# Modulation products in four column quarters at once, and indivisible blocks of matmuls, in a two-block transformer kernel

## The chip, the cores and the metric

The kernel runs on one core of one Trainium2 chip. The metric is device time in microseconds (us) of one execution. The core's engines work side by side from instruction lists of their own: TensorE (PE, matmuls; its weight loads are shown as PEld), VectorE (DVE), ScalarE (ACT), GpSimd (POOL) and SyncE (SP, which here issues all transfers). They wait for each other through semaphores.

## The reference

The program chains two blocks of two layers each on 512 tokens of width 1024. What matters here are three parts of it:

```python
# first block, second layer: stick-breaking attention, 16 heads of 64
logits = einsum('bhtd,bhsd->bhts', q, k) * SCALE
log_keep = where(mask, log_sigmoid(-logits), 0)
later = cumsum(log_keep, reverse=True) - log_keep
a = where(mask, exp(log_sigmoid(logits) + later), 0)
out = einsum('bhts,bhsd->bhtd', a, v)

# second block, both layers: modulation from two condition vectors c and c_ctx
m = silu(cvec) @ ada_w[i] + ada_b[i]            # (1024) x (1024, 3072)
shift, scale, gate = split(m, 3)

# second block, first layer: latent attention, 16 heads, 512 tokens + 256 context tokens
p = softmax(einsum('bqhgd,bkhd->bhgqk', q, k) * scale)
o = einsum('bhgqk,bkhv->bqhgv', p, v)
```

All values are float32.

## The kernel before

The whole program is unrolled: `layer0`, `layer1`, `mla` and `diff` are traced one after the other into five instruction lists. A scheduler of the framework then orders each engine's list by its own estimate of when operands are ready and sets all semaphores; so the order on an engine is not that of the Python text. Tiles come from pools; a tag with `bufs=n` has n buffers, and whoever takes a buffer waits for the last reader of its earlier content.

PSUM has one bank `mm` (`p_mm`) and one bank `pv` (`p_pv`) in the stages spoken of here, two `tr` banks for transposes (`p_tr`), and two double banks `lg` for logits (`p_lg`). Weights arrive in three buffers of 512 KB with the tag `wraw`; ACT rounds one into a high part `wh`, POOL subtracts to get the low part `wl` (lines 126 and 127), and most products run as three matmuls (lines 147 to 149).

Two stages carry the change. In the **stick stage** (`layer1`, `stick_steps`) `pipeline` walks through 24 steps, three for each pair of heads c: logits on PE (lines 684 to 686), sigmoids on ACT, a running product on DVE (line 695), a product on POOL (line 698), and two steps later transposes on PE (`aT_p`, line 172) and, at each pair's third step, the products of probabilities and values: eight float32 matmuls (line 726), which alternate between the lower and the upper 64 columns of the PE array (e = 0 and 1) and accumulate in `pv`. In the **latent stage** (`mla`, `mla_steps`) there are 80 steps, five for each head: logits (lines 147 to 149), softmax over ACT, DVE and POOL (lines 1073 to 1075 and 1036), transposes (`PT_p`), and after every second head the products with the values for both heads: 12 matmuls 64x512, then 4 matmuls 64x256 into `pv` again (line 1057), with the same two column halves in turn. Between the steps `pipeline` puts pieces of other work, gates and projections that use `mm` among them.

The modulation vectors are such pieces. There are six parts q (three for each layer of the second block), three in each stage. A part takes eight blocks k of 128 weight rows. `ada_piece` loads one block (`araw`, 512 KB, a `wraw` buffer) and multiplies it with the 32 columns of `cs[:, k, :]`, two of which hold the condition vectors, in two float32 matmuls of 512 columns (line 768). Even blocks use column quarters 0 and 1 of the PE array, odd ones 2 and 3; all eight blocks accumulate in one `pv` bank. DVE copies the bank to SBUF once (line 772), and small matmuls with `asel` add the quarters (line 775). In the trace each float32 matmul that is no transpose has two records of one form.

Of the kernel before, what the change touches and what calls it, by code (L numbers as in the profile page):

```python
# [10 lines left out]
F32 = mybir.dt.float32  # L11
F32R = mybir.dt.float32r
BF16 = mybir.dt.bfloat16
AF = mybir.ActivationFunctionType
ALU = mybir.AluOpType
# [4 lines left out]
P = 128  # L20
# [3 lines left out]
NT = S // P  # L24
# [5 lines left out]
FREE = 10 ** 6  # L30
# [11 lines left out]
class Block:  # L42
    def __init__(self, ctx, tc, a, out):
        self.ctx, self.tc, self.nc, self.a, self.out = ctx, tc, tc.nc, a, out
        self.nc.scalar.preload_act_table_set("natural_log_exp_and_others")
        self.st = ""
        self.last_pair = None
        self.pools = {}
        self.open_pools = {}
        self.cp = self.open("consts")  # L50
        self.wp = self.open("weights")
        self.sm = self.open("small")
        self.ps = self.open("psum", space=PSUM)
        self.dr = ctx.enter_context(tc.tile_pool(name="scratch", bufs=1, space=DRAM))
        self.xs = self.dr.tile([S, D], F32, name="xs")
        self.xs2 = self.dr.tile([S, D], F32, name="xs2")
        self.xf = self.dr.tile([NK, P, S], F32, name="xf")
        self.gates = self.dr.tile([2, 2, 2, 512], F32, name="gates")
        self.wq = []
        self.w_dma = self.w_split = self.w_next = 0  # L60
# [465 lines left out]
    def layer1(self):  # L526
        nc, a = self.nc, self.a
# [9 lines left out]
        ks, qs, vtok = [], [], [lp.tile([P, D], F32, name=f"vtok{t}") for t in range(NT)]  # L537
# [16 lines left out]
        og, pieces, steps = {}, [], []  # L554
# [12 lines left out]
        for c in range(NK):  # L567
            pieces.append((c + 1, lambda c=c: z_piece(c), 3 * c + 3))
        for q in range(3):
            n = 6 * q + 3  # L570
            pieces += self.ada_pieces(q, [n + k // 2 for k in range(8)])
        for c in range(NK):
            steps += self.stick_steps(c, ks, qs, vtok, og, ap)
        self.pipeline(steps, 2, pieces)
# [69 lines left out]
    def stick_steps(self, c, ks, qs, vtok, ogs, pool):  # L644


        nc = self.nc
# [54 lines left out]
        def second(n, segs):  # L702
            aT, bt = h["aT"], h["bt", n]
            b0, pr = 0, None
            for e, i, o in segs:
                if b0 + i + 1 > 4:
                    b0, pr = 0, None
                if pr is None:
                    pr = self.p_tr("aT_p")
                for j in range(i + 1):  # L710
                    self.transpose(pr[:, (b0 + j) * P:(b0 + j + 1) * P], bt[:, o + j * P:o + (j + 1) * P])
                src = pr[:, b0 * P:(b0 + i + 1) * P].rearrange("p (j t) -> p j t", t=P)
                if i == 3:
                    nc.scalar.copy(aT[e][:, 3 * i:4 * i + 1, :], src)
                else:
                    nc.vector.tensor_copy(out=aT[e][:, 3 * i:4 * i + 1, :], in_=src)
                b0 += i + 1
            if n < 2:
                return
            self.need(c + 1)  # L720
            pv = self.p_pv("pv1")
            for j in range(NT):
                for e in range(2):
                    hd = 2 * c + e
                    av = aT[e][:, 4 * j:10 + j:3, :]
                    nc.tensor.matmul(pv[64 * e:64 * e + 64, j * P:], lhsT=vtok[j][:, hd * 64:(hd + 1) * 64], rhs=av, start=(j == 0), stop=(j == NT - 1))
            og = ogs[c // 2][:, (c % 2) * 512:(c % 2 + 1) * 512]
            nc.vector.tensor_tensor(out=og, in0=pv, in1=og, op=ALU.mult)

# [2 lines left out]
        self.last_pair = h  # L732
        tiles = [[(0, 3, 0), (0, 2, 512), (0, 0, 896)], [(1, 3, 0), (1, 2, 512), (1, 0, 896)], [(0, 1, 0), (1, 1, 512)]]
        return [(lambda n=n, t=t: first(n, t), lambda n=n, t=t: second(n, t)) for n, t in enumerate(tiles)]


# [16 lines left out]

    def ada_pieces(self, q, steps):

        return [(FREE, lambda k=k: self.ada_piece(q, k), n) for k, n in enumerate(steps)]

    def ada_piece(self, q, k):
        nc = self.nc
        layer, part = divmod(q, 3)  # L760
        if k == 0:
            self.ada_ps = self.p_pv("ada_p")
        ps = self.ada_ps
        raw = self.wp.tile([P, 1024], F32, tag="wraw", name="araw", bufs=3)
        nc.sync.dma_start(out=raw, in_=self.a["ada_w_2"][layer, k * P:(k + 1) * P, part * 1024:(part + 1) * 1024])
        for b in range(2):
            j = 2 * (k % 2) + b
            nc.tensor.matmul(ps[32 * j:32 * j + 32, :], lhsT=self.cs[:, k, :], rhs=raw[:, b * 512:(b + 1) * 512], start=(k < 2), stop=(k >= 6), tile_position=(0, 32 * j))  # L768
        if k < 7:
            return  # L770
        row = self.wp.tile([P, 1024], F32R, tag="wh", name="ada_row", bufs=4).bitcast(F32)
        nc.vector.tensor_copy(out=row[:, :512], in_=ps)
        pr = self.p_tr("ada_t")
        for t in range(4):
            nc.tensor.matmul(pr[:, 4 * t:4 * t + 4], lhsT=row[:, t * P:(t + 1) * P], rhs=self.asel, start=True, stop=True)
        b0 = self.col["ada_b"] + 8 * q
        for v in range(2):
            nc.vector.tensor_tensor(
                out=self.ada[:, v, 8 * q:8 * q + 8].rearrange("p (b t) -> p b t", t=4),
                in0=pr[:, :16].rearrange("p (t b v) -> p v b t", b=2, v=2)[:, v],  # L780
                in1=self.vec[:, b0:b0 + 8].rearrange("p (b t) -> p b t", t=4), op=ALU.add)
        if part == 1:
            nc.vector.tensor_scalar(out=self.ada1[:, :, 8 * layer:8 * layer + 8], in0=self.ada[:, :, 8 * q:8 * q + 8], scalar1=1.0, scalar2=None, op0=ALU.add)
        if part == 2:
            pr = self.p_tr("ada_g")
            nc.tensor.matmul(pr[:4, :], lhsT=self.asel, rhs=row[:, :512], start=True, stop=True)
            nc.vector.tensor_copy(out=row[:4, 512:], in_=pr[:4, :])
            for b in range(2):
                nc.sync.dma_start(out=self.gates[layer, :, b], in_=row[2 * b:2 * b + 2, 512:])
# [48 lines left out]
    def mla(self):  # L838
        nc, a = self.nc, self.a
# [12 lines left out]
        raws = [p0.tile([P, 768], F32, tag="lraw", name="lraw", bufs=3) for _ in range(3)]  # L852
# [44 lines left out]
        V = lambda g, ns: [(8 * g + 1, lambda i=i: self.mla_v(g, i, grp, kvlat, self.pools["mla1"]), n) for i, n in enumerate(ns)]  # L897
# [20 lines left out]
        pieces, steps = [], []  # L918
        pieces = V(0, [0, 1, 2])
        for g in range(4):  # L920
            n = 20 * g
# [1 line left out]
            if g < 3:  # L923
                pieces += V(g + 1, [n + 6, n + 7, n + 9]) + K(2 * g + 2, n + 10, n + 11) + Q(g + 1, [n + 12, n + 13, n + 14, n + 14, n + 15, n + 16])
        for q in range(3, 6):
            pieces += self.ada_pieces(q, [20 * q - 38 + k for k in range(8)])
        self.chain = []
        for h in range(16):
            steps += self.mla_steps(h, grp, kTs, og, ogc, pool)
# [68 lines left out]
    def mla_steps(self, h, grp, kTs, og, ogc, pool):  # L998
        nc = self.nc
        g, hh, e = h // 4, h % 4, h % 2  # L1000
        H = {}
# [39 lines left out]
        def second(qb):  # L1041
            for pe, dst, i in H[qb]:
                self.probs_T(pe, dst, i)
            if qb < 4:
                return
            if e == 0:
                return
            c = h // 2
            H0 = H["prev"]
            self.need(8 * g + 1)  # L1050
            V = grp["V", g]
            for nk, n, k0, px, o in ((6, 512, 0, "pt", og[c]), (2, 256, 4, "ptc", ogc[c])):
                pv = self.p_pv("pv2")[:, :n]
                for k in range(nk):
                    for ee, HH in ((0, H0), (1, H)):
                        vs = slice((hh - 1 + ee) * 64, (hh + ee) * 64)
                        nc.tensor.matmul(pv[64 * ee:64 * ee + 64, :], lhsT=V[:, k0 + k, vs], rhs=HH[px][:, k, :], start=(k == 0), stop=(k == nk - 1))  # L1057
                nc.vector.tensor_tensor(out=o, in0=pv, in1=o, op=ALU.mult)

        if self.chain:  # L1060
            self.chain[-1]["next"] = prep
            H["prev"] = self.chain[-1]
        self.chain.append(H)
        return [(lambda q=q: first(q), lambda q=q: second(q)) for q in range(5)]

    def soft(self, L, pool, W, bufs):
# [432 lines left out]
```

## Time and profile before

| | |
|---|---|
| runs of the kernel before | 1595.2, 1595.64 (median), 1601.13 us |
| the profiled execution's own time | 1594.69 us |
| its span, first to last instruction | 1592.9 us |
| PE, DVE, ACT, POOL busy | 95%, 58%, 46%, 38% of the span |
| stick stage with the pieces (383 to 547 us) | 164 us, PE busy 148.44 us |
| latent stage with the pieces (787 to 1057 us) | 270 us, PE busy 265.76 us |
| mean granted TensorE clock | 0.983 of full speed |

Times in the rows are counted from the span's start. A matmul's record begins where its data start to stream and ends at a modelled end, so records of neighbours overlap: what a matmul costs is read from one start to the next, and a run of like matmuls from its total busy time. An engine that is not busy may just have nothing to do; only a wait on the engine that ends the stage costs time.

### The profile page before, as it was taken

How to read it: one execution, taken by the hardware profiler on the slowest of the kernel's cores; microseconds unless marked ns; L12 is line 12 of the kernel's file. 1: busy time of each engine (PE TensorE's matmuls, PEld its weight loads, DVE VectorE, ACT ScalarE, POOL GpSimd, SP SyncE). 2: the span in 40 equal slices, each digit the busy share in tenths (PEclk: the TensorE clock that was granted, in tenths of full speed). 3: DMA queues.
4: the chain of work that ended last, by engine and by line, in shares of the span. 5: the costliest groups of instructions: out<-in, count | busy, mean ns of one | idle time of the engine just before them, and what ended most of it. 6: DMA issues, size and time to landing. Idle time of an engine off the chain costs nothing.

```text
span 1592.9 us, 24439 instructions
## 1 busy us (share of the span) xinstructions
PE 1505.3 (95%) x9590; PEld 1253.3 (79%) x9590; DVE 927.9 (58%) x1769; ACT 733.8 (46%) x1347; POOL 603.4 (38%) x431
## 2 busy tenths in 40 slices
PE   6999999999899899999999999999798999999997
PEld 4777889997555678888876657579697999999987
DVE  6676465523766656442465566546866555556576
ACT  5323344436566433332565455543235554555642
POOL 2534555553444453212333222435442324343310
PEclk9999999999999999999999999999898999999999
DMA  5322432223244334311103030425421112111122
GB/s 157 105 79 89 123 118 83 98 84 115 81 132 133 106 120 124 87 44 50 50 1 120 5 120 2 145 80 186 132 69 55 41 41 67 40 56 52 54 74 100
DMA packets 149747, 136.01 MB, mean 85 GB/s; under 512 B 12612, under 2 KB 135224, under 8 KB 149632
## 3 DMA queue, kind: packets, MB, share of 16 engines
q1 hardware_dynamic: 149632, 134.45, 27.3%
q8 instruction: 76, 1.25, 0.3%
q14 instruction: 39, 0.32, 0.1%
HBM read 126.02 MB, written 8.40 MB: 84 GB/s over the span
## 4 chain that ended last, share of the span: by engine, by line
PE 41%; DVE 6%; ACT 5%; issue 3%; DMA 2%; POOL 1%; SPq 0%; DVEq 0%; POOLq 0%; ACTq 0%
PE PT_p L172 5%; PE pv L1057 4%; PE qkv_p L147 2%; PE qkv_p L149 2%; PE qkv_p L148 2%; PE pv L1420 2%; PE gt_p L147 2%; PE gt_p L148 2%; PE gt_p L149 2%; PE lg L147 2%; PE lg L148 2%; PE lg L149 2%; PE ada_p L768 1%; ACT pe L1074 1%; DMA wraw<-in_out_w_dram 1%
## 5 line engine op out<-in xcount | busy, mean ns | idle before, releaser
L127 POOL TENSOR_TENSOR wl<-wraw,wh 128x1024 fp32r<-128x1024 f32 (+2 forms) x159 | 376.4, 2376 | 379.5 <-ACT wh L126 366.3
L126 ACT CAST wh<-wraw 128x1024 fp32r<-128x1024 f32 (+2 forms) x164 | 166.4, 1020 | 281.2 <-issue 57.9
L1074 ACT ACTIVATE pe<-lg,st 128x768 f32<-128x768 f32 x160 | 130.5, 816 | 76.7 <-DVE st L1073 60.6
L1073 DVE TENSOR_REDUCE st<-lg 128x1 f32<-128x768 f32 x160 | 133.9, 845 | 38.4 <-PE lg L1401 20.1
L1036 POOL TENSOR_SCALAR pe<-pe,st 128x768 f32<-128x768 f32 (+1 forms) x96 | 73.6, 767 | 159.2 <-DVE st L1075 154.0
L147 PE MATMUL qkv_p<-wh,h 128*128 128x256 f32 x384 | 109.9, 286 | 0.8 <-ACT V L1346 0.7
L172 PEld LDWEIGHTS PT_p<-ident,pe 128*128 128x128 f32 x640 | 72.3, 142 | 47.8 <-issue 16.5
L149 PE MATMUL qkv_p<-wh,h 128*128 128x256 f32 x384 | 108.6, 283 | 0.2 <-DVE h L217 0.2
L148 PE MATMUL qkv_p<-wl,h 128*128 128x256 f32 x384 | 108.7, 283 | 0.0
L172 PE MATMUL PT_p<-ident,pe 128*128 128x128 f32 x640 | 99.9, 282 | 8.0 <-DVE pe L1406 3.0
L1405 POOL TENSOR_SCALAR pe<-pe,st 128x768 f32<-128x768 f32 x32 | 29.2, 912 | 126.2 <-DVE st L1404 80.3
L147 PE MATMUL out_p<-wh,o 128*128 128x256 f32 x256 | 74.7, 293 | 0.9 <-DVE y L1272 0.8
L147 PEld LDWEIGHTS qkv_p<-wh,h 128*128 128x128 f32 x384 | 73.1, 190 | 3.0 <-ACT V L1346 1.3
L148 PE MATMUL out_p<-wl,o 128*128 128x256 f32 x256 | 74.0, 291 | 1.3 <-POOL wl L127 1.3
L149 PE MATMUL out_p<-wh,o 128*128 128x256 f32 x256 | 73.7, 291 | 0.1
L149 PEld LDWEIGHTS qkv_p<-wh,h 128*128 128x128 f32 x384 | 73.0, 190 | 0.4 <-DVE h L217 0.4
L148 PEld LDWEIGHTS qkv_p<-wl,h 128*128 128x128 f32 x384 | 73.2, 191 | 0.0
L147 PE MATMUL kv_p<-wh,kv 128*128 128x256 f32 x256 | 72.1, 282 | 1.2 <-ACT kv L219 1.2
L148 PE MATMUL kv_p<-wl,kv 128*128 128x256 f32 x256 | 71.6, 280 | 0.0
L149 PE MATMUL kv_p<-wh,kv 128*128 128x256 f32 x256 | 71.1, 280 | 0.0
L698 POOL TENSOR_TENSOR sb_b<-sb_b,sb_k 128x1023 f32<-128x1023 f32 (+1 forms) x32 | 43.0, 1354 | 64.7 <-DVE sb_k L695 36.7
L695 DVE TENSOR_TENSOR_SCAN sb_k<-sb_k 128x512 f32<-128x512 f32 (+3 forms) x64 | 61.7, 1007 | 7.6 <-ACT sb_k L690 7.3
(456 smaller groups left out, 4568.1 us busy)
## 6 DMA issues: line engine op xcount, KB each, us to landing
araw<-in_ada_w_dram SPq DMA_DIRECT2D x48, 512.0 KB
wraw<-in_diff_w_in_dram SPq DMA_DIRECT2D x32, 512.0 KB
wraw<-in_out_w_dram SPq DMA_DIRECT2D x24, 512.0 KB
wraw<-in_a_w_in_dram SPq DMA_DIRECT2D x16, 512.0 KB
wraw<-in_ple_gate_w_dram SPq DMA_DIRECT2D x16, 512.0 KB
wraw<-in_w_kv_dram SPq DMA_DIRECT2D x16, 512.0 KB
wraw<-in_b_w_in_dram SPq DMA_DIRECT2D x16, 512.0 KB
wraw<-in_mla_w_in_dram SPq DMA_DIRECT2D x11, 512.0 KB
```

What stands on the lines that cost most here:

```text
L126: nc.scalar.copy(h[:, :n], raw[:, :n])
L127: (nc.vector if i < 3 or pool == "ow3" else nc.gpsimd).tensor_tensor(out=l[:, :n], in0=raw[:, :n], in1=h[:, :n].bitcast(F32), op=ALU.subtract)
L147: mm(out, lhsT=lh, rhs=rh, start=start, stop=False)
L148: mm(out, lhsT=lh, rhs=rl, start=False, stop=False)
L149: mm(out, lhsT=ll, rhs=rh, start=False, stop=stop)
L172: self.nc.tensor.transpose(out, in_, self.ident[:in_.shape[0], :in_.shape[0]])
L695: nc.vector.tensor_tensor_scan(out=kp[:, rev], data0=kp[:, rev], data1=kp[:, rev], initial=1.0, op0=ALU.mult, op1=ALU.min)
L698: nc.gpsimd.tensor_tensor(out=bt[:, o:o + w - 1], in0=bt[:, o:o + w - 1], in1=kp[:, o + 1:o + w], op=ALU.mult)
L1036: nc.gpsimd.tensor_scalar(out=pe, in0=pe, scalar1=st[:, 1:2], scalar2=0.0, op0=ALU.mult, op1=ALU.add)
L1057: nc.tensor.matmul(pv[64 * ee:64 * ee + 64, :], lhsT=V[:, k0 + k, vs], rhs=HH[px][:, k, :], start=(k == 0), stop=(k == nk - 1))
L1073: nc.vector.tensor_reduce(out=st[:, 0:1], in_=L, axis=AX.X, op=ALU.max, negate=True)
L1074: nc.scalar.activation(pe, L, AF.Exp, bias=st[:, 0:1], accum_out=st[:, 2:3])
```

## The change

Two things are done. First, `ada_piece` takes two blocks at a time (four pieces for each part instead of eight): their four matmuls use the four column quarters, each is a sum of its own (`start` and `stop` both true), and the result goes to an `mm` bank instead of `pv`; DVE copies the first of the four into the SBUF row and adds the other three to it. The loads become pieces of their own, one step earlier (`ada_load`). Second, the four matmuls of such a piece, the eight of a pair in the stick stage, and the 12 and the 4 of two heads in the latent stage each stand in `tc.tile_critical()`, which keeps a block of instructions together. That makes 24 + 8 + 16 = 48 blocks. Line numbers behind `__init__` move by 1 to 21.

```diff
@@ __init__
+        self.araw = {}
@@ layer1
         for q in range(3):
-            n = 6 * q + 3
-            pieces += self.ada_pieces(q, [n + k // 2 for k in range(8)])
+            n = 6 * q + 4
+            pieces += self.ada_pieces(q, [n, n + 1, n + 3, n + 4])
@@ stick_steps, second
-            for j in range(NT):
-                for e in range(2):
-                    ...
-                    nc.tensor.matmul(pv[64 * e:64 * e + 64, j * P:], ...)
+            with self.tc.tile_critical():
+                for j in range(NT):
+                    for e in range(2):
+                        ...
+                        nc.tensor.matmul(pv[64 * e:64 * e + 64, j * P:], ...)
@@ ada_pieces, ada_load, ada_piece
-        return [(FREE, lambda k=k: self.ada_piece(q, k), n) for k, n in enumerate(steps)]
+        pieces = []
+        for k, n in enumerate(steps):
+            pieces += [(FREE, lambda k=k: self.ada_load(q, k), n - 1), (FREE, lambda k=k: self.ada_piece(q, k), n)]
+        return pieces
+
+    def ada_load(self, q, k):
+        layer, part = divmod(q, 3)
+        raws = self.araw[q, k] = []
+        for i in (2 * k, 2 * k + 1):
+            raws.append(self.wp.tile([P, 1024], F32, tag="wraw", name="araw", bufs=3))
+            self.nc.sync.dma_start(out=raws[-1], in_=self.a["ada_w_2"][layer, i * P:(i + 1) * P, part * 1024:(part + 1) * 1024])
 
     def ada_piece(self, q, k):
         if k == 0:
-            self.ada_ps = self.p_pv("ada_p")
-        ps = self.ada_ps
-        raw = self.wp.tile([P, 1024], F32, tag="wraw", name="araw", bufs=3)
-        nc.sync.dma_start(out=raw, in_=...)
-        for b in range(2):
-            j = 2 * (k % 2) + b
-            nc.tensor.matmul(ps[32 * j:32 * j + 32, :], lhsT=self.cs[:, k, :], rhs=raw[:, b * 512:(b + 1) * 512], start=(k < 2), stop=(k >= 6), tile_position=(0, 32 * j))
-        if k < 7:
+            self.arow = self.wp.tile([P, 1024], F32R, tag="wh", name="ada_row", bufs=4).bitcast(F32)
+        row = self.arow
+        ps = self.p_mm("ada_p")
+        raws = self.araw.pop((q, k))
+        with self.tc.tile_critical():
+            for i, raw in enumerate(raws):
+                for b in range(2):
+                    j = 2 * i + b
+                    nc.tensor.matmul(ps[32 * j:32 * j + 32, :], lhsT=self.cs[:, 2 * k + i, :], rhs=raw[:, b * 512:(b + 1) * 512], start=True, stop=True, tile_position=(0, 32 * j))
+        if k == 0:
+            nc.vector.tensor_copy(out=row[:, :512], in_=ps)
+        else:
+            nc.vector.tensor_tensor(out=row[:, :512], in0=ps, in1=row[:, :512], op=ALU.add)
+        if k < 3:
             return
-        row = self.wp.tile([P, 1024], F32R, tag="wh", name="ada_row", bufs=4).bitcast(F32)
-        nc.vector.tensor_copy(out=row[:, :512], in_=ps)
@@ mla
         for q in range(3, 6):
-            pieces += self.ada_pieces(q, [20 * q - 38 + k for k in range(8)])
+            pieces += self.ada_pieces(q, [20 * q - 38 + 2 * k for k in range(4)])
@@ mla_steps, second
-                for k in range(nk):
-                    for ee, HH in ((0, H0), (1, H)):
-                        ...
+                with self.tc.tile_critical():
+                    for k in range(nk):
+                        for ee, HH in ((0, H0), (1, H)):
+                            ...
```

What the built program makes of it shows in PE's list. The first place is the first modulation piece of the stick stage. Before, the matmuls of three blocks stand one behind the other there, each block behind the semaphore of its own transfer:

```order
L149 MATMUL z_p<-b,wl 128x512
L768 MATMUL ada_p<-araw,cs 32x512 [waits DMAHW5_49]
L768 MATMUL ada_p<-araw,cs 32x512
L768 MATMUL ada_p<-araw,cs 32x512 [waits DMAHW6_49]
L768 MATMUL ada_p<-araw,cs 32x512
L768 MATMUL ada_p<-araw,cs 32x512 [waits DMAHW7_49]
L768 MATMUL ada_p<-araw,cs 32x512
L147 MATMUL z_p<-b,wh 128x512 [waits DVE_49]
```

In the changed program the same place holds the four matmuls of two blocks, and around them instructions that do no arithmetic (line 781 is the `with` line):

```order
L150 MATMUL z_p<-b,wl 128x512
L781 NO_OP [waits DMAHW5_49,DMAHW6_49,DVE_49,Activation_49]
L1516 UNCONDITIONAL_BRANCH [waits DMAHW2_49,DMAHW1_49,DMAHW3_49,DMAHW0_49,DMAHW4_49,PE_sequencer_49,DMAHW5_49,DVE_49,DMAHW6_49,PE_49,DMAHW7_49,Activation_49,Pool_49]
L785 MATMUL ada_p<-araw,cs 32x512 x4
L781 UNCONDITIONAL_BRANCH
L781 NO_OP [waits PE_49,PE_sequencer_49]
L685 MATMUL sb_l<-K_3545,Q_3541 128x512 [waits DVE_49,PE_49,Activation_49]
```

The branch into the block waits for 13 semaphores: the eight of the transfers, those of DVE, ACT and POOL, and PE's own two. Their values are the counts that stand in the program up to this point, so every instruction and every transfer that the scheduler put ahead of the block has to have ended. The branch out of the block is followed by a wait for PE's own matmuls to end. All 48 blocks have this form, and the other engines' lists get a branch without a wait at the same places.

The second place is the first product with the values in the latent stage, for heads 0 and 1 (`pv_7129` before, `pv_7187` in the change). Before, 11 of its 12 matmuls stand in three groups, the first (one matmul) further ahead:

```order
L172 MATMUL qT_p<-ident,qs 96x128
L1057 MATMUL pv_7129<-PT,V 64x512 x2
L147 MATMUL kb_p<-kvlat,wh 128x256 [waits DVE_49]
L148 MATMUL kb_p<-kvlat,wh 128x256
L149 MATMUL kb_p<-kvlat,wl 128x256
L1057 MATMUL pv_7129<-PT,V 64x512 x2
L172 MATMUL PT_p<-ident,pe 128x128 [waits DVE_49,Pool_49]
L172 MATMUL PT_p<-ident,pe 128x128
L172 MATMUL PT_p<-ident,pe 128x128 [waits DVE_49,Pool_49]
L172 MATMUL PT_p<-ident,pe 128x128
L1057 MATMUL pv_7129<-PT,V 64x512 x7
L149 MATMUL lg_7149<-kTs_5790,qT_6924 128x512
```

In the changed program the 12 stand in one piece behind such a branch:

```order
L1074 NO_OP [waits PE_sequencer_49,DVE_49,Activation_49]
L150 MATMUL lg_7211<-kTs_5848,qT_6982 128x512
L1516 UNCONDITIONAL_BRANCH [waits DMAHW2_49,DMAHW1_49,DMAHW3_49,DMAHW0_49,DMAHW4_49,PE_sequencer_49,DMAHW5_49,DVE_49,DMAHW6_49,PE_49,DMAHW7_49,Activation_49,Pool_49]
L1078 MATMUL pv_7187<-PT,V 64x512 x12
L1074 UNCONDITIONAL_BRANCH
L148 MATMUL lg_7211<-kTs_5848,qT_6982 128x256 [waits PE_49]
L1074 NO_OP [waits PE_sequencer_49]
L149 MATMUL lg_7211<-kTs_5848,qT_6982 128x256
```

What moved: the groups of line 1057 became one, and a wait for all other engines stands ahead of it.

## Rows read from the trace of the kernel before

**Rows 1.** The page, sections 1 and 3: engines and instruction transfers

```profile
span 1592.9 us, 24439 instructions
...
PE 1505.3 (95%) x9590; PEld 1253.3 (79%) x9590; DVE 927.9 (58%) x1769; ACT 733.8 (46%) x1347; POOL 603.4 (38%) x431
...
q8 instruction: 76, 1.25, 0.3%
```

**Rows 2.** Busy time by engine in the stick and the latent stage

```profile
core 0: us, PE busy (x) PEld busy (x) DVE busy (x) ACT busy (x) POOL busy (x), PEclk, DMA share, GB/s
383.00:547.00 164.00, 148.44 (x830) 94.20 (x828) 113.59 (x168) 99.99 (x144) 77.25 (x49) 0.97 0.33 106
787.00:1057.00 270.00, 265.76 (x1534) 174.01 (x1532) 163.22 (x398) 151.30 (x344) 88.93 (x111) 0.99 0.19 60
```

**Rows 3.** The same view for the modulation matmuls alone (line 768)

```profile
383.00:547.00 164.00, 18.70 (x96) 2.76 (x96) 0.97 0.33 106
787.00:1057.00 270.00, 25.25 (x96) 3.46 (x96) 0.99 0.19 60
```

**Rows 4.** The same for the latent products with values (line 1057)

```profile
787.00:1057.00 270.00, 64.61 (x256) 17.41 (x256) 0.99 0.19 60
```

**Rows 5.** The same for the stick products with values (line 726)

```profile
383.00:547.00 164.00, 24.82 (x128) 12.04 (x128) 0.97 0.33 106
```

**Rows 6.** Timeline of PE (start, us): modulation matmuls of one block

```profile
394.11 1.05 PE L768 MATMUL ada_p<-araw,cs 128*32 128x512 f32 x4
```

**Rows 7.** Timeline of PE, 438 to 441 us: a run on four quarters

```profile
439.08 1.06 PE L768 MATMUL ada_p<-araw,cs 128*32 128x512 f32 x8
```

**Rows 8.** Timeline of PE, 803 to 813 us: one latent product in pieces

```profile
804.78 1.08 PE L1057 MATMUL pv<-PT,V 128*64 128x512 f32 x4
...
806.38 3.65 PE L1057 MATMUL pv<-PT,V 128*64 128x512 f32 x14
...
811.09 1.08 PE L1057 MATMUL pv<-PTc,V 128*64 128x256 f32 x8
```

**Rows 9.** Timeline of PE near 414 us: one stick product in one run

```profile
414.52 2.37 PE L726 MATMUL pv<-aT,vtok 128*64 128x512 f32 x16
```

**Rows 10.** Line 172 on PE: its wait instructions (ns min/median/max)

```profile
L172 PEldq EVENT_SEMAPHORE  x171: 51/51/583, 2.1 to 1541.6; - x171
```

**Rows 11.** Groups by line, stick stage: busy us, mean ns, idle before

```profile
L695 DVE TENSOR_TENSOR_SCAN sb_k<-sb_k 128x512 f32<-128x512 f32 (+3 forms) x64 | 61.7, 1007 | 7.6 <-ACT sb_k L690 7.3
L698 POOL TENSOR_TENSOR sb_b<-sb_b,sb_k 128x1023 f32<-128x1023 f32 (+1 forms) x32 | 43.0, 1354 | 64.7 <-DVE sb_k L695 36.7 <-ACT sb_b L691 10.2 <-ACT Q L670 8.3
...
L127 POOL TENSOR_TENSOR wl<-wraw,wh 128x1024 fp32r<-128x1024 f32 x9 | 22.0, 2451 | 9.1 <-ACT wh L126 9.1
```

**Rows 12.** Groups by line, latent stage

```profile
L1073 DVE TENSOR_REDUCE st<-lg 128x1 f32<-128x768 f32 (+1 forms) x90 | 69.7, 774 | 17.0 <-PE lg L149 16.0 <-POOL wl L127 0.4
L1074 ACT ACTIVATE pe<-lg,st 128x768 f32<-128x768 f32 (+1 forms) x91 | 68.9, 757 | 40.3 <-DVE st L1073 31.7 <-DVE st L1075 4.0 <-POOL pe L1036 3.8
```

**Rows 13.** Timeline of all engines, 848 to 852 us

```profile
848.79 0.96 DVE L1073 TENSOR_REDUCE st<-lg 128x1 f32<-128x768 f32 x1 [1.15 <-PE lg L149]
...
848.96 1.05 PE L768 MATMUL ada_p<-araw,cs 128*32 128x512 f32 x4
...
851.12 0.91 ACT L1074 ACTIVATE pe<-lg,st 128x768 f32<-128x768 f32 x1
...
851.46 1.05 PE L768 MATMUL ada_p<-araw,cs 128*32 128x512 f32 x4
```

**Rows 14.** Timeline near 413 us: a weight transfer and the cast behind it

```profile
412.74 0.38 SPq L116 DMA_DIRECT2D wraw<-in_b_w_in_dram  x1
...
416.88 1.04 ACT L126 CAST wh<-wraw 128x1024 fp32r<-128x1024 f32 x1 [0.53 <-DMA wraw<-in_b_w_in_dram]
```

**Rows 15.** Busy time by engine and granted clock, 420 to 440 us

```profile
420.00:440.00 20.00, 15.60 (x77) 10.55 (x75) 12.51 (x16) 8.03 (x12) 7.28 (x5) 0.83 0.17 53
```

**Rows 16.** Tile ada_p: the copy out of PSUM, ns

```profile
L772 DVE COPY ada_row<-ada_p x6: 665/692/692, 413.5 to 1013.9; 128x512 f32<-128x512 f32 x6
```

More of the change, by code (lines that the diff above doesn't have):

```diff
@@ L721, in second @@
             pv = self.p_pv("pv1")
-            for j in range(NT):
-                for e in range(2):
-                    hd = 2 * c + e
-                    av = aT[e][:, 4 * j:10 + j:3, :]
-                    nc.tensor.matmul(pv[64 * e:64 * e + 64, j * P:], lhsT=vtok[j][:, hd * 64:(hd + 1) * 64], rhs=av, start=(j == 0), stop=(j == NT - 1))
+            with self.tc.tile_critical():
+                for j in range(NT):
+                    for e in range(2):
+                        hd = 2 * c + e
+                        av = aT[e][:, 4 * j:10 + j:3, :]
+                        nc.tensor.matmul(pv[64 * e:64 * e + 64, j * P:], lhsT=vtok[j][:, hd * 64:(hd + 1) * 64], rhs=av, start=(j == 0), stop=(j == NT - 1))
             og = ogs[c // 2][:, (c % 2) * 512:(c % 2 + 1) * 512]
@@ L761, in ada_piece @@
         if k == 0:
-            self.ada_ps = self.p_pv("ada_p")
-        ps = self.ada_ps
-        raw = self.wp.tile([P, 1024], F32, tag="wraw", name="araw", bufs=3)
-        nc.sync.dma_start(out=raw, in_=self.a["ada_w_2"][layer, k * P:(k + 1) * P, part * 1024:(part + 1) * 1024])
-        for b in range(2):
-            j = 2 * (k % 2) + b
-            nc.tensor.matmul(ps[32 * j:32 * j + 32, :], lhsT=self.cs[:, k, :], rhs=raw[:, b * 512:(b + 1) * 512], start=(k < 2), stop=(k >= 6), tile_position=(0, 32 * j))
-        if k < 7:
+            self.arow = self.wp.tile([P, 1024], F32R, tag="wh", name="ada_row", bufs=4).bitcast(F32)
[12 more added lines that the diff above has]
+        if k < 3:
             return
-        row = self.wp.tile([P, 1024], F32R, tag="wh", name="ada_row", bufs=4).bitcast(F32)
-        nc.vector.tensor_copy(out=row[:, :512], in_=ps)
         pr = self.p_tr("ada_t")
@@ L1053, in second @@
                 pv = self.p_pv("pv2")[:, :n]
-                for k in range(nk):
-                    for ee, HH in ((0, H0), (1, H)):
-                        vs = slice((hh - 1 + ee) * 64, (hh + ee) * 64)
-                        nc.tensor.matmul(pv[64 * ee:64 * ee + 64, :], lhsT=V[:, k0 + k, vs], rhs=HH[px][:, k, :], start=(k == 0), stop=(k == nk - 1))
+                with self.tc.tile_critical():
+                    for k in range(nk):
+                        for ee, HH in ((0, H0), (1, H)):
+                            vs = slice((hh - 1 + ee) * 64, (hh + ee) * 64)
+                            nc.tensor.matmul(pv[64 * ee:64 * ee + 64, :], lhsT=V[:, k0 + k, vs], rhs=HH[px][:, k, :], start=(k == 0), stop=(k == nk - 1))
                 nc.vector.tensor_tensor(out=o, in0=pv, in1=o, op=ALU.mult)
```

## The prediction, made before the change was timed

> **What bounds the kernel now.** First the page: PE is busy for 95% of the span, the others for 38 to 58% [rows 1]. Then the two stages that hold the edited lines: PE is busy for 148.44 of 164 us in the stick stage and for 265.76 of 270 us in the latent stage; DVE, the next, for 113.59 and 163.22 [rows 2]. So in both PE ends the stage; its idle time there is 15.6 + 4.2 = 19.8 us. Then the edited matmuls alone: line 768 takes 18.70 + 25.25 = 43.95 us [rows 3], line 1057 64.61 us [rows 4], line 726 24.82 us [rows 5]. Together 133 us of PE: what the change can win lies in these, and what it can lose lies in how PE enters and leaves the 48 blocks.
>
> **What it removes.** Modulation: one block of weights (four records on two quarters) takes 1.05 us [rows 6], two blocks on four quarters, where the scheduler happened to put them together, 1.06 us [rows 7]. The quarters run side by side, so the second block is free. After the change all 24 pieces have that form: 24 x 1.06 = 25.4 us, 18.5 us less.
>
> Latent products: a run of four records (two matmuls that share the halves) takes 1.08 us, one of 14 records (three pairs and a single) 3.65 us [rows 8]; so a pair, or a single that runs alone, costs (3.65 - 1.08) / 3 = 0.857 us, and each run 0.22 us once. Twelve matmuls in one piece are 6 x 0.857 + 0.22 = 5.36 us, the four of the context 1.08 us as now [rows 8]: 8 x 6.44 = 51.5 us, 13.1 us less than [rows 4]. Stick products: an undivided run takes 2.37 us [rows 9], eight make 19.0, 5.8 us less than [rows 5]; but the longer runs of before hold waits for DVE's copies inside them, and these don't go. I take 3, with 0 and 5.8 as bounds. Sum removed: 18.5 + 13.1 + 3 = 34.6 us, bounds 31.6 and 37.4.
>
> **What it adds on PE.** The order shows a branch with 13 waits into every block, and behind the block a branch and a wait for PE's own end. No such wait for everything stands in the trace of before; I bound it by its parts.
>
> The fixed part: a wait instruction on PE takes 51 ns [rows 10]. A block brings about a dozen instructions without arithmetic; those ahead of the one that blocks are covered, some six are not: 0.3 us. PE has to run empty twice, at the entry and at the exit; the nearest price is the 0.22 us that a run costs beyond its pairs [rows 8], so 0.44. Together 0.74 us, 48 x 0.74 = 35.5 us. Bounds: 0.3 (the emptying falls into waits that PE has anyway), 14 us; 1.2 (all twelve on the path, and twice 0.3), 58 us.
>
> The wait for the other engines: what the scheduler put ahead of a block has just been started there when PE arrives, so the nearest row is the instruction under way. When the modulation matmuls of 848.96 us start, DVE has 0.79 us of a maximum to go (848.79 + 0.96); at 851.46 ACT has 0.57 us of an exponential to go [rows 13]. Before, PE passed both. In the latent stage these instructions average 0.77 and 0.76 us [rows 12]; with half of one to go, and the later of several engines counting, I take 0.5 us for the 28 blocks there: 14 us. In the stick stage DVE's scans average 1.01 us and POOL's instructions 1.35 and 2.45 us [rows 11]; 1.0 us for the 20 blocks there: 20 us. Bounds: nothing left to go, 0; a whole one each time, 28 x 0.96 + 20 x 2.45 = 76 us.
>
> The wait for transfers: the 512 KB that SP issues at 412.74 us release the cast that waits for them at 416.88 us, 4.1 us later [rows 14]. Before, PE waits for its own block's transfer alone; now also for weights that are needed only later. Going through the changed lists with matmuls at their start-to-start times, I estimate that some 20 of the 48 blocks have a transfer ahead of them that is less than 2 us old. With part of its rest hidden behind the engines' wait I take 1.2 us more for each: 24 us; bounds 0 and 20 x 3 = 60 us. Sum added: 35.5 + 34 + 24 = 93.5 us, 1.95 us for each block.
>
> **What it moves elsewhere.** DVE gets 18 more reads of PSUM at 0.69 us [rows 16], 12.4 us. I cost them at nothing: DVE is free for 50 us of the stick stage and 107 of the latent one [rows 2], and PE goes on meanwhile. The cover ends where the next user of `mm` follows at once: then its first matmul waits for the add, at most 12.4 us in all. That the modulation no longer holds `pv` for eight blocks frees the first stick product of each part; its price is within the idle time below. SP issues the same 48 loads, two together. Behind a PE that stands at a branch are the transposes and logits of the running step; DVE, ACT and POOL wait for these next, and having caught up they give part of the loss back: PE's later waits become shorter. At most they vanish, 19.8 us by [rows 2]; I take 20 off, with 0 and 40 as bounds, since modelled ends can hide short waits.
>
> **Sum.** 93.5 - 34.6 - 20 = 38.9 us slower. The profiled execution took 1594.69 us, 0.95 us below the median of the runs shown, so about 1634; since 20 us of absorbed waits is only what the rows show openly, I forecast 1632 us.
>
> **A page's price.** The Trainium skill, Advanced Engine Details and Errata, Control Flow Timing, gives about 51 ns for an unconditional branch. By it PE's 96 added branches would be an estimated 4.9 us. No run here shows a branch yet; the 0.3 us of the fixed part comes from [rows 10] and doesn't use it.
>
> **The rivals.**
>
> Faster: the entry costs little, because the other engines and transfers are mostly done where the scheduler put the blocks. The place is PE's branch into a block; the point that decides is the whole price of a block. The change pays below (34.6 + 20) / 48 = 1.14 us with the absorbed waits, below 34.6 / 48 = 0.72 us without. With only 0.74 us fixed and nothing else: 35.5 - 34.6 - 20 = -19, 1576 us; with 0.5 us of waiting on top 1600. For it: in the latent stage ACT, DVE and POOL are idle for 107 to 181 of 270 us [rows 2], and the transfers take 19% of their engines' time. Against it: both instances of [rows 13] have an engine at work. Chance 0.20 for a gain over 0.5%.
>
> No change to be measured: the price is near 1.0 to 1.3 us for each block. 0.5% (8 us) is about what a measurement of this kernel can tell from no change. Chance 0.10.
>
> Much slower: each taken branch on PE stops its instruction stream until a new piece of instructions has come. The transfers of instructions took 0.3% of 16 engines' 1592.9 us for 76 packets [rows 1], 1.0 us each; 96 of them on top of the forecast give 1632 + 96 = 1728 us. For it: the trace of before has no branch within the program, so nothing shows that they are cheap. Against it: in PE's list the target of every branch is the next instruction, which the engine has probably fetched already. Chance 0.06. The Trainium skill, Runtime: NRT & Kernel Launch, Instruction fetch mechanics, warns that a taken branch whose target lies outside the prefetched window stalls for a fetch. By that rule most of these branches, which go to the next instruction, would stay inside; the trace can't show it.
>
> The clock: where PE was busy for only 15.6 of 20 us, the granted clock was 0.83 for these 20 us [rows 15], that is part of the time at 1.2 instead of 2.4 GHz. More standing still on PE can bring more of this in the stick stage. Ten such stretches would be some 10 x 0.17 x 20 = 34 us; this belongs to the upper end, not to a case of its own.
>
> **Chances and range.** Slower by over 0.5%: 0.64 for the forecast and its neighbourhood, 0.06 for the branches, 0.70 together. Within 0.5%: 0.10. Faster: 0.20. The range reaches down to the middle of the faster case, 1580, since cases of both signs share the chance, and up to 1692: added parts at 1.3 times my values with no waits absorbed are 122 - 35 = +87, and the clock takes some more. The forecast's own range is 1605 to 1690.
>
> **What would show it.** Line 785's busy time near 25 us and line 1078's near 51 us would show the removed part right. The added part would show as PE idle ahead of the first matmul of lines 785, 729 and 1078, some 1 to 2 us in the median, ended by DVE, ACT, POOL or a transfer, and as shorter idle time between the records behind the blocks. PE's idle time in the two stages should grow from 20 to 90 us or more, while its busy time falls. I am wrong if the first matmuls of the blocks follow their predecessors within 0.5 us, which would mean that the branch finds everything done; or if PE's idle time ahead of each block is 3 us and more with nothing to release it, which would be the instruction stream.

## The result, and the profile of the changed kernel

The changed kernel takes 1716.18 us (median of 4 runs, 1710.93 to 1719.32) against 1595.42 us (4 runs of before beside it): ratio 1.0748, 95% interval 1.0705 to 1.0791. It is slower, as forecast, but by 121 us instead of 37, and lies outside the range. Page, sections 1 and 3 [rows 1]:

```profile
span 1709.1 us, 25083 instructions
...
PE 1526.1 (89%) x9590; PEld 1276.2 (75%) x9590; DVE 923.5 (54%) x1787; ACT 733.8 (43%) x1347; POOL 601.3 (35%) x431
...
q8 instruction: 78, 1.28, 0.3%
```

Busy time by engine and granted clock in the stick and the latent stage, which have moved to 383 to 620 and 860 to 1172 us [rows 2]:

```profile
383.00:620.00 237.00, 171.30 (x828) 108.60 (x827) 111.19 (x177) 99.92 (x141) 77.56 (x50) 0.80 0.24 76
860.00:1172.00 312.00, 265.31 (x1525) 183.54 (x1524) 160.81 (x405) 144.72 (x328) 88.71 (x110) 0.93 0.16 52
```

The two stages are 73 and 42 us longer, 115 of the 116 us by which the span grew. PE stands still for 65.7 + 46.7 = 112.4 us of them, 19.8 before. And the granted clock has fallen from 0.97 and 0.99 to 0.80 and 0.93: it has two levels, so 2 x 0.20 x 237 = 95 us and 2 x 0.07 x 312 = 44 us were spent at 1.2 GHz.

The groups of the three edited lines and of the two that wait behind them (busy us, mean ns, idle time ahead and what ended it):

```profile
L785 PE MATMUL ada_p<-araw,cs 128*32 128x512 f32 x192 | 31.3, 726 | 40.1 <-DMA araw<-in_ada_w_dram 11.7 <-DVE og L731 7.9 <-DMA wraw<-in_out_w_dram 5.3
L729 PE MATMUL pv<-aT,vtok 128*64 128x512 f32 (+3 forms) x128 | 31.1, 651 | 14.3 <-DMA wraw<-in_b_w_out_dram 10.1 <-ACT sb_k L691 1.8 <-ACT aT L715 1.0
L1078 PE MATMUL pv<-PT,V 128*64 128x512 f32 x192 | 43.0, 596 | 5.7 <-ACT qT L1032 4.3 <-DVE PTc L1113 0.8 <-DVE qT L1033 0.6
L1078 PE MATMUL pv<-PTc,V 128*64 128x256 f32 x64 | 8.8, 391 | 6.2 <-ACT PT L1111 2.7 <-PEq L1074 1.9 <-ACT pe L1095 0.6
L685 PE MATMUL sb_l<-K,Q 128*128 128x512 f32 (+3 forms) x64 | 31.7, 495 | 18.8 <-DVE K L665 18.4 <-DVE QL L673 0.4
L686 PE MATMUL sb_l<-K,QL 128*128 128x512 f32 (+3 forms) x64 | 28.6, 447 | 8.5 <-ACT QL L674 7.0 <-PEq L781 0.7
```

The first four rows are the 48 blocks, from here on called sections: 40.1 + 14.3 + 5.7 + 6.2 = 66.3 us of idle time at their entries. Most of it is ended by work that the section doesn't need. A modulation product waits for the weights of `out_w`, a stick product for those of `b_w_out`; and by the times of issue and landing in the records, all four waits for `araw` (11.7 us) end with a load that only the next section uses. Line 1078 is busy for 51.8 instead of 64.6 us [rows 4], as forecast. Line 785 takes 31.3 instead of 43.95 us [rows 3], more than the 25.4 forecast, and line 729 rose from 24.82 [rows 5] to 31.1: eight of the 24 and six of the eight sections there run at half clock, wholly or in part. Two timelines of PE show this, a section at half clock and then a step of the stick stage (start, us):

```profile
441.83 4.02 PE L729 MATMUL pv<-aT,vtok 128*64 128x512 f32 x16 [0.91 <-ACT sb_k L691]
```

The product that took 2.37 us [rows 9] takes 4.02: the stretch 434.95 to 445.19 us has a granted clock of 0.50. The step, PE and DVE:

```profile
459.53 1.07 PE L785 MATMUL ada_p<-araw,cs 128*32 128x512 f32 x8 [0.85 <-ACT sz L208]
...
462.10 2.38 DVE L696 TENSOR_TENSOR_SCAN sb_k<-sb_k 128x512 f32<-128x512 f32 x3
...
464.51 0.68 DVE L665 TENSOR_TENSOR K<-kT_p,K 64x512 fp32r<-64x512 f32 x1
...
465.34 0.48 PE L685 MATMUL sb_l<-K,Q 128*128 128x512 f32 x1 [2.69 <-DVE K L665]
```

Three scans stand ahead of K in DVE's order, and PE, 2 us behind a section's end, has nothing else to issue. Before, the same three scans stand ahead of K, but PE has other matmuls meanwhile:

```profile
445.45 2.39 DVE L695 TENSOR_TENSOR_SCAN sb_k<-sb_k 128x512 f32<-128x512 f32 x3 [1.09 <-ACT sb_k L690]
...
447.23 1.05 PE L768 MATMUL ada_p<-araw,cs 128*32 128x512 f32 x4
447.87 0.68 DVE L664 TENSOR_TENSOR K<-kT_p,K 64x512 fp32r<-64x512 f32 x1
```

These waits of the logits for K and QL come in six of the changed stage's steps, 25.4 us; before, line 684 waited 1.6 us.

**One account for all kernels.** To compare runs I split the time from the first matmul of the stick stage's gate (`z_p`) to the last stick product, and from the first latent logits to the last latent product, into three parts. Idle is length less PE's busy time. Clock is half of the busy time that lay in stretches at 1.2 GHz: what these records took longer than at 2.4 GHz. Work is the rest, PE's work as at 2.4 GHz. The parts of the program that no kernel here changes confirm it: 224.0 to 224.7 us of work between the two stages and 479.2 to 480.9 behind them in every kernel.

| kernel | median us | both stages | work | idle | clock |
|---|---|---|---|---|---|
| before | 1595.4 | 451.1 | 425.1 | 19.8 | 6.2 |
| changed | 1716.2 | 567.3 | 399.0 | 111.9 | 56.4 |
| 1 change without sections | 1609.7 | 460.6 | 424.2 | 29.7 | 6.7 |
| 2 sections on modulation only | 1672.1 | 523.1 | 406.6 | 74.5 | 42.1 |
| 3 sections on products only | 1652.3 | 501.3 | 412.9 | 68.1 | 20.3 |
| 4 48 sections that merge nothing | 1748.5 | 603.0 | 432.8 | 114.4 | 55.8 |
| 5 quarters kept together by order | 1605.2 | 460.2 | 408.5 | 41.1 | 10.6 |
| 6 the same, products by priority | 1606.3 | 459.8 | 410.3 | 39.5 | 10.0 |
| 7 changed, entries filled | 1716.1 | 568.8 | 450.1 | 86.4 | 32.4 |
| 8 as 5, with bank mm and adds | 1609.9 | 465.2 | 408.2 | 41.3 | 15.8 |
| 9 before, products whole by order | 1583.3 | 435.2 | 408.8 | 24.9 | 1.5 |
| 10 as 9, quarters in the latent stage | 1588.0 | 438.2 | 398.8 | 33.2 | 6.2 |
| 11 as 5, products whole by order | 1590.8 | 447.7 | 390.5 | 41.1 | 16.1 |
| 12 changed, order for sections | 1595.3 | 447.8 | 393.5 | 40.0 | 14.1 |

The changed kernel less before: work -26.1, idle +92.1, clock +50.2, together +116.2 us. The stretch ahead of the stages, which nothing changes, took from 377.7 to 385.4 us in these profiles, so a difference of a few us in one profile says little.

### The profile page after: what moved, and what is told of

Read it like the earlier page. It is cut to its first block, busy times and chain, and to the rows that moved or that the text cites. A ratio compares the mean times of both kernels' runs of the same rounds, so it can differ in the third digit from the quotient of the medians.

```text
span 1709.1 us, 25083 instructions
## 1 busy us (share of the span) xinstructions
PE 1526.1 (89%) x9590; PEld 1276.2 (75%) x9590; DVE 923.5 (54%) x1787; ACT 733.8 (43%) x1347; POOL 601.3 (35%) x431
## 5 line engine op out<-in xcount | busy, mean ns | idle before, releaser
L173 PE MATMUL PT_p<-ident,pe 128*128 128x128 f32 x640 | 103.7, 285 | 13.5 <-DVE pe L1427 3.6
L173 PEld LDWEIGHTS PT_p<-ident,pe 128*128 128x128 f32 x640 | 76.2, 146 | 35.3 <-issue 11.9
L699 POOL TENSOR_TENSOR sb_b<-sb_b,sb_k 128x1023 f32<-128x1023 f32 (+1 forms) x32 | 42.3, 1331 | 140.9 <-DVE sb_k L696 102.7
L785 PE MATMUL ada_p<-araw,cs 128*32 128x512 f32 x192 | 31.3, 726 | 40.1 <-DMA araw<-in_ada_w_dram 11.7
```

Of the source, the lines that this page charges most:

```text
L173: self.nc.tensor.transpose(out, in_, self.ident[:in_.shape[0], :in_.shape[0]])
L699: nc.gpsimd.tensor_tensor(out=bt[:, o:o + w - 1], in0=bt[:, o:o + w - 1], in1=kp[:, o + 1:o + w], op=ALU.mult)
```

## The experiments

**Theory 1:** a section's entry waits for everything on every engine and queue, and the idle time brings the half clock. Against it: the quarters lower the clock (2), branches (3), loads of the modulation issued just ahead (4), the bank and the adds (5). Rivals 6 to 9 are told in the expectations of their runs.

**1. The change without sections.** Three times:

```
-with self.tc.tile_critical():
+if True:
```

> The changed kernel with all 48 critical sections taken out, the rest as it is: modulation two weight blocks at a time in four quarters, loads in pairs, sums added in SBUF, bank mm. Theory 1 (the wait for every engine and transfer at a section's entry idles PE, and the idle time brings the half clock): nothing is left of the loss; modulation is 18.5 us of PE cheaper, the products of probabilities and values cost what they did before, so 1573 to 1585 us, with half clock in the two stages back at 10 to 20 us from 140. Rival 2 (the four quarters themselves, or their 32-column matmuls, make the clock fall): half clock in the two stages stays above 50 us and the time above 1610. Rival 5 (modulation in bank mm waits for DVE's adds): 1595 to 1615, PE idle ahead of line 785 and of the next user of mm.

1609.72 us, ratio 1.0092 (1.0067 to 1.0117). The 106 us between it and the changed kernel go with the sections, and the clock is that of before. But instead of theory 1's gain it is 14.5 us slower than before. The scheduler took the quarters apart again: of the 24 groups 12 are whole, and line 785 is busy for 42.8 us, so this run can't settle rival 2. Idle time grew by 9.9 us, with 4.7 us of waits for `ada_row`, as rival 5 has it, and 5.1 more for K.

**2 and 3. Half of the sections each.** The section kept at the modulation alone, and, on the kernel before, put around the two products alone.

> The changed kernel with the 24 sections around the modulation products alone; the products of probabilities and values may be split by the scheduler again. Theory 1: a section costs what it costs in the changed kernel, 93 us of idle time and 50 us of clock over 48, so 2.98 us each: 24 x 2.98 - 18.5 = +53, about 1649 us (1630 to 1665). Rival 2 (clock by the quarters): as the changed kernel in its half clock, 1650 or more. Rival 4 (the waits are for loads issued just ahead, thus for the modulation's own pairs of 1 MB): nearly all of the loss is here, 1680 or more.

> The kernel before with critical sections around the 24 products of probabilities and values alone (8 in the stick stage, 16 in the latent one); modulation as before. Theory 1: 24 x 2.98 less 13 to 16 us for whole products: +56, about 1652 us (1630 to 1665). Rival 4 (loads of the modulation): near 1595, since these sections have no load of their own. Rival 2 (clock by the quarters): half clock in the two stages stays near 15 us, and the time is about 1595 - 15 + 24 x 1.9 = 1626.

1672.09 us (1.0477, 1.0455 to 1.0498) and 1652.28 us (1.0345, 1.0317 to 1.0373). The second fell where theory 1 put it; rival 4 falls with it, since its sections have no load of their own. The first is 7 us above theory 1's bound. Idle time grew by 54.7 and 48.3 us, 2.3 and 2.0 us for each of 24 sections; work fell by 18.5 and 12.2. Run 3 has no merged quarters and still loses 14 us more to the clock than before, which rival 2 doesn't explain.

**4. Sections that merge nothing.** The kernel before with this edit:

```
+        with self.tc.tile_critical():
         for b in range(2):
             j = 2 * (k % 2) + b
             nc.tensor.matmul(ps[32 * j:32 * j + 32, :], ...)
```

> The kernel before with a critical section around each pair of modulation matmuls, as they are: 48 sections, that merge nothing and leave the computation's steps as before. Theory 1: 48 x 2.98 = +143 us, 1738 (1690 to 1760), PE's idle time at the entries ended by DVE, ACT, POOL or a transfer. Rival 3 (branches and instruction fetch): the same for each section, but constant, without a releaser, and the same in both stages; if only that counted, the idle time of an entry would hardly vary. The forecast's own sizes (1.95 us a section, no clock): +93, 1689.

1748.54 us (1.0965, 1.0938 to 1.0992): +153 against +143. Its group:

```profile
L769 PE MATMUL ada_p<-araw,cs 128*32 128x512 f32 x192 | 64.0, 752 | 92.7 <-DMA araw<-in_ada_w_dram 29.6 <-issue 18.8 <-ACT pe L1075 6.7
```

The entries vary from 0.44 to 4.46 us. Six of the 48 take 0.44 us, whichever engine the profile names: this is the floor, which holds the last of the wait records, 51 ns, and a branch record of 171 ns. Behind the section it is 0.1 us. So rival 3 falls: a constant price is there, but small. 18.8 us here ("issue", 9 entries) have no releaser in the profile. No transfer of instructions lies in them, and six of them end 4.1 to 4.6 us after a load was issued, about as late as the load of [rows 14] landed. A wait for these loads is likely, but not shown.

**5 and 8. Quarters kept together by order.** No section; the block that is loaded second comes first, each matmul is pinned in issue order behind the one ahead:

```
+        with self.tc.high_priority():
+            for i in (1, 0):
                 for b in range(2):
                     j = 2 * i + b
+                    m = nc.tensor.matmul(...)
+                    if first is not None:
+                        self.tc.keep_in_program_order(m)
+                    first = m
```

> No critical section. Modulation two weight blocks at a time in four quarters, kept together by the order alone: the four matmuls have a raised priority in the scheduler, the block that is loaded second comes first, and each is pinned in issue order behind the one ahead of it. The sum stays in the bank pv over the four steps as in the kernel before (no adds on DVE). Products of probabilities and values as before. Theory 1 (only the sections' waits cost; keeping the quarters together is worth what it was costed at): the 18.5 us of PE work go and nothing comes, 1577 us (1570 to 1585), half clock in the two stages as before (14 us). Rival 2 (quarters lower the clock): half clock above 50 us, 1610 or more. Rival 6 (four matmuls that need two loads wait for the second one): idle time ahead of them of 10 us or more, ended by a transfer, 1585 to 1595.

> As the first of this list (four quarters kept together by order, no section), but with the changed kernel's data flow: each piece in a bank of mm, taken to SBUF and added by DVE. It differs from the first by the bank and the adds alone. The forecast's step (DVE's 18 adds are covered, 0 us): the same as the first, 1577. Rival 5 (a PE that comes back to the bank waits for the add; 4.7 us of that were seen in the changed kernel without its sections): 5 to 12 us above the first, 1582 to 1590, PE idle ended by DVE's ada_row.

1605.15 us (1.0065, 1.0042 to 1.0087) and 1609.91 us (1.0093, 1.0069 to 1.0116): both miss theory 1's 1577, and the first rival 6's range too. Here all 24 groups are whole, and half clock takes 24 and 34 us, below the 50 of rival 2, which falls. The quarters cost what was forecast:

```profile
L785 PE MATMUL ada_p<-araw,cs 128*32 128x512 f32 x192 | 26.4, 624 | 16.0 <-DMA araw<-in_ada_w_dram 16.0
```

Work fell by 16.6 us, but idle time grew by 21.3: four matmuls wait for two loads (rival 6, 16.0 us where before showed none), and in the stick stage the waits for DVE's K and aT grew from 7.0 to 19.1. So the merged work paid for itself in neither. The second, with the bank and the adds, lies 4.8 us above the first, just under rival 5's 5 to 12. Runs 11 and 12 below differ in the same two things and lie 4.5 us apart; each difference of the means is about 2.5 times its standard error. So the 18 adds and the bank, with the order that follows from them, cost some 4 to 5 us. Idle time is the same (41.1 and 41.3), and only 1.2 us of it in run 8 is ended by `ada_row`; where the rest goes, one profile of each can't tell.

**6. Products by priority.** The loops of both products in `with self.tc.high_priority():`.

> As the run before it in this list, and the products of probabilities and values of both stages get the raised priority too, so that the scheduler leaves them whole without a section. Theory 1: another 12 us of PE work go (what the section around them took off in the kernel with product sections alone), 1565 us (1556 to 1576). Rival 7 (whole products cost PE the filling that covered waits on DVE and ACT): the work falls, but idle time grows by as much, 1573 to 1585.

1606.33 us (1.007, 1.0049 to 1.0091): theory 1's 1565 is missed and nothing gained, but not by rival 7; the work itself didn't fall. The timeline of one product:

```profile
877.21 1.07 PE L1079 MATMUL pv<-PT,V 128*64 128x512 f32 x2
...
886.35 5.36 PE L1079 MATMUL pv<-PT,V 128*64 128x512 f32 x22
```

The first head is ready earlier, and its first matmul runs alone. The other 22 records then take as long as a whole product's 24.

**7. Entries filled.** The changed kernel with this ahead of each section (results unused):

```
+for _ in range(2):
+    self.tc.keep_in_program_order(nc.tensor.matmul(pv[:, :256],
+        lhsT=self.ident, rhs=self.cs.rearrange("p k n -> p (k n)"), ...))
```

> The changed kernel with two matmuls more ahead of each of its 48 sections (fp32, 128 rows by 256 columns, into the section's own bank, which the section then overwrites; they compute nothing that is used), pinned behind what stands ahead of them on PE: an estimated 0.87 us of PE work for each section, from 1.05 us for a modulation block of 512 columns. 42 us of work are added; the idle time ahead of the sections, 66 us now, can take 36 of it. Theory 1 with its second half (idle time on PE brings the half clock): PE stands still less, the half clock in the two stages falls from 140 to under 70 us, and the time falls although work was added: 1690 us (1675 to 1705) against 1716. Rival 8 (the sections as such bring the half clock, by emptying PE, not the length of the wait): half clock as in the changed kernel, 1716 to 1730. Rival 9 (what the entry waits for is started by PE's last instructions, so the wait only moves behind the added work): idle time stays near 66 us, 1740 to 1760.

1716.09 us, as the changed kernel; theory 1's 1690 missed. The two stages:

```profile
382.70:606.20 223.50, 177.05 (x933) 117.06 (x930) 117.90 (x179) 103.92 (x148) 78.45 (x50) 0.92 0.27 81
832.80:1178.00 345.20, 305.31 (x1724) 212.32 (x1724) 171.69 (x425) 157.78 (x353) 93.20 (x116) 0.95 0.15 48
```

51 us more work, 25.5 us less idle time, 24 us less lost to the clock: half clock fell from 140 to 72 us with the same 48 sections. Rival 8 falls; rival 9 holds in part, since the entries kept 56 of their 66 us. Most of the 25.5 came from waits outside them; the logits' waits for K and QL fell from 25.4 to 0.2 us. So with PE standing still less there is less half clock, as theory 1 has it, though the filling cost as much as it gave. The run adds work and takes idle time away at once, and doesn't tell the two apart.

**9 and 10. Whole products by order, on the kernel before.** The same in both products:

```
-                    for ee, HH in ((0, H0), (1, H)):
+                    for ee, HH in ((1, H), (0, H0)):
```

with the raised priority and the pin of run 5. Run 10 has the pinned pairs of run 5 in the latent stage besides.

> The kernel before with the products of probabilities and values kept whole by their order alone, no section, modulation untouched: of each pair of halves the one that is ready later (the second head) comes first, each matmul is pinned in issue order behind the one ahead of it, and they have the raised priority. In the run with whole products by priority alone the first head's first matmul still ran by itself, 1.07 us, and the rest took 5.36 us, as long as the whole product takes (5.37). Theory 1 (the products are cheaper whole, and only the sections cost): 64.6 us of the latent products become 51.5 and 24.8 of the stick products 19 to 22, -16 us: 1579 (1572 to 1588). Rival 7 (the matmul that ran ahead filled a wait, so that idle time grows by what the work falls): 1590 to 1598.

> As the run before it in this list, and in the latent stage alone the modulation in pairs of blocks on four quarters, kept together by order, the sum in the bank pv. Theory 1: another 9 us of PE work go in the stage where PE is nearly the only bound: 1570 (1562 to 1580). Rival 6 (four matmuls wait for two loads; 7.6 us ended by the modulation's transfer in this stage in the first run with pairs): 1576 to 1584.

1583.32 us (0.9918, 0.9896 to 0.994), as theory 1 forecast, and 1587.95 us (0.9946, 0.9924 to 0.9967), where theory 1's 1570 is missed: it is a little over rival 6's range. In run 9 all products are whole:

```profile
L1064 PE MATMUL pv<-PT,V 128*64 128x512 f32 x192 | 43.0, 596 | 0.5 <-ACT PT L1100 0.5
L728 PE MATMUL pv<-aT,vtok 128*64 128x512 f32 (+3 forms) x128 | 19.0, 439 | 2.9 <-DVE aT L716 2.9
L1064 PE MATMUL pv<-PTc,V 128*64 128x256 f32 x64 | 8.7, 392 | 0.9 <-DVE PTc L1102 0.9
```

They take 51.7 and 19.0 us, with 4.3 us of waits ahead of them. Run 10 takes 10 us of work more away, but 8.3 us come back as idle time, 8.0 of it ended by loads of `araw`, and 4.7 us by the clock. So the pairs lose in the latent stage too, 4.6 us by the medians.

**11 and 12. Everything by order.** Run 5 with run 9's products, and the changed kernel's data flow (bank mm, adds) with order in place of all sections.

> Pairs of blocks on four quarters in both stages (sum in the bank pv) and whole products, all by order, no section. Theory 1: the first run with pairs, 1605, less the 16 us of the products: 1589 (1580 to 1597), since in the stick stage the pairs' gain went into waits for DVE and loads. If it comes to 1570 or less, the loss of the first run with pairs was chance of its order.

> The changed kernel's data flow whole (pairs of blocks, bank mm, adds on DVE, products of probabilities and values undivided) with order and priority in place of all 48 sections. What is left between it and the changed kernel are the sections alone. Theory 1: PE's work in the two stages at full clock is that of the changed kernel, 399 us (a little more where one group is still taken apart), idle time 40 us as in the other runs without sections, half clock 15 to 30 us: 1590 (1580 to 1600), so the sections cost 126 us of the changed kernel's 1716. Rival (undivided groups and the data flow are what costs, not the sections): 1640 or more.

1590.77 us (0.9967, 0.9945 to 0.9988) and 1595.29 us (0.9992, 0.9975 to 1.0008), both as theory 1 has it. Run 12's stages:

```profile
379.60:557.50 177.90, 150.36 (x854) 99.33 (x852) 120.35 (x179) 105.93 (x152) 78.16 (x50) 0.92 0.32 100
783.90:1053.70 269.80, 257.26 (x1613) 182.51 (x1613) 171.69 (x425) 163.07 (x365) 93.78 (x116) 0.99 0.20 62
```

One group of quarters and one product are still taken apart. Between it and the changed kernel lie the sections, and the orders that follow from them and from the pins: 1716.18 - 1595.29 = 121 us, 2.5 us a section. By the account 71.9 us of it is idle time, 42.3 us clock and 5.5 us work.

## Why the prediction was wrong

**Removed work: right in kind, somewhat too high.** 34.6 us were forecast; 26.1 went in the changed kernel, 31.6 in run 12. Pieces of 1.07 us and whole products of 5.37 + 1.08 us came as worked out. What they replaced was smaller than I took it. Counted from one start to the next, at full clock (worked out from the records), the modulation matmuls took 41.2 us before and 24.9 in the change, the latent products 60.7 and 51.7, the stick products 22.2 and 18.8; the other matmuls took 2.7 us more. So the latent term was 9 us, not 13.1: the busy time of pieces, which I took, counts stretches in which a neighbour's record runs too. My 3 us for the stick products was near.

**Added waits: the mechanism right, the size a little high.** I had 93.5 us. The entries are 66.3 us, the idle time behind the sections 7.1 (worked out from the records of 48 sections), 73 together, 1.5 us a section instead of 1.95. In runs 2, 3 and 4 the same sum is 2.1, 1.9 and 2.0 us a section. The parts fit less well than their sum. The fixed part is 0.44 + 0.1, not 0.74. Transfers end 9 entries, not 20, but with 3.3 us each, 29.7 us instead of 24. ACT and DVE end 36 with 33.7 us, in which the fixed part is contained; I had 34 beside it.

**Absorbed waits: the first step that failed.** I took 20 us off, because engines that have caught up would shorten PE's later waits. They don't: PE's idle time outside entries and exits is 19.8 us before, 24.7, 22.4 and 16.3 in runs 2, 3 and 4, and 38.5 in the changed kernel, 19 us more than before instead of 20 less. There the logits' waits for K and QL alone grew by 24 us. That is not a price of each section: these waits are 5.1 and 1.9 us in runs 2 and 3, none in run 4 with 24 sections in the stick stage, 0.2 in run 7 with the same 48 sections and filled entries, and 6.6 in run 12 without sections. It goes with the order that the scheduler made of this kernel: in the step shown above, PE has nothing left to issue while DVE gets to K. What in the changed kernel brings this order about, no run shows.

**The clock: the second, and the larger.** The prediction named ten stretches of 20 us at 0.83, 34 us, and left them to the upper end, "not to a case of its own". It is 50.2 us, in both stages. The row that showed it [rows 15] had PE idle for 4.4 of 20 us. A forecast that adds 1.95 us of idle time 48 times to 451 us of both stages makes such a share of idle time the rule. With all four terms as measured, -26 + 73 + 19 + 50, the sum comes to 116; without the 20 us by which the added waits came out lower, the miss would have been larger still. PE's busy time in the two stages, which I expected to fall, rose from 414 to 437 us, by the half clock.

**The rivals.** Faster needed a section below 1.14 us; it costs 1.5 in idle time alone. The branches: two instruction transfers more than before (78 against 76), and 48 branch records on PE of 171 ns in the median, 8 us in all. The Trainium skill, Runtime: NRT & Kernel Launch, Instruction fetch mechanics, has a stall only for targets outside what was fetched ahead; the two transfers for 48 sections agree. That DVE's adds cost nothing did not hold: 4 to 5 us, by runs 5 and 8 and runs 11 and 12.

## What to carry to other kernels

A section that keeps a few matmuls together is paid for at its entry, where PE waits for all engines and all queues, and then once more by the clock: here 2.5 us against 31.6 / 48 = 0.7 us of work saved. Keep matmuls together by their order instead: put the operand that is ready last first, and pin the rest behind it (run 9, 12 us faster than before, with a one-line swap as its core). Work taken from PE is not yet time gained, where loads and other engines are as close as here: the whole products of run 9 took 16 us of work away and gained 12, but with the pairs, which wait for two loads, runs 5 and 11 took 17 and 35 us away; the first lost 11 us, the second gained 5.

## What the runs showed of the hardware

Two halves of the columns run side by side (two matmuls 1.08 us [rows 8], one alone 1.07), so one matmul that goes ahead alone costs its full 1.07 us and saves nothing later (22 records 5.36 us, 24 records 5.37 us). The granted clock goes with PE's standing still: the four kernels with 75 to 114 us of idle time in the stages lose 32 to 56 us to it, those below 45 us lose 1.5 to 16. It is not the sum alone: runs 2 and 3 have 75 and 68 us of idle time and lose 42 and 20, and why they differ is not settled.
